# A three-stage network on one core: small tiles widened so that the large buffers begin at multiples of 512 bytes

## The chip, the cores and the metric

The kernel runs on one core of a Trainium2 chip. The metric is the device time in microseconds of one execution; less is better. One execution was also recorded by the profiler, and the lines below come from that record.

## The reference

The reference computes one network of two blocks on 256 tokens of 1024 channels, all in f32. Cut to what matters:

```python
# first block
h = rmsnorm(x, g_mix); proj = h @ w_in                     # 1024 -> 7168 columns
y_a = (rg_lru(xa, forward) + rg_lru(xa, reverse)) * gelu(a_gate) @ w_a_out
z = gate * fftconv(z, k, filt_bias)                        # twice, then @ w_b_out
x = x + (g_a * y_a + g_b * y_b) @ w_o
vals, idx = lax.top_k(softmax(rmsnorm(x) @ w_router).T, 32)
ye = (silu(xe @ w_gate) * (xe @ w_up)) @ w_down            # 16 experts, 1024 -> 2048 -> 1024
x = rmsnorm(x + scatter_add(ye * vals), g_final)
# second block, two layers, each:
x = x + 0.5 * swiglu(x)                                    # 1024 -> 2816 -> 1024
x = x + mixer(x)                                           # recurrent heads, attention heads, pooling
x = x + cross_attention(x, mem)
x = x + 0.5 * swiglu(x)
```

## The kernel before, in words

**Layout of the work.** Tokens or channels lie on the 128 partitions. A weight matrix is read from memory in chunks of 128 rows by 2048 f32 numbers, 8,192 bytes for each partition, in the order in which the products use them. Each chunk is one transfer, issued from SyncE, and it arrives in a buffer named `wc`. Outside the experts, ScalarE rounds the chunk to a high part `wh` (line 303), VectorE subtracts to get the low part `wl` (line 304), and TensorE makes three products of the parts (line 457 with the weights as the moving operand, line 422 with them as the stationary one).

**Stages.** The first block's mixer runs to about 400 us. The experts follow: 16 experts read 24 chunks each, without the split, into 18 buffers in turn (`RING2`): eleven slots of the mixer's pool that are free by then, four `ring` buffers, and three pairs of `wh` and `wl` taken as halves (a row is 4,096 bytes there). Line 1006 makes the gate and up products, line 1030 the down product, lines 1039 to 1043 add the result to `x`. The second block runs from about 1320 us to the end: gated networks with line 457, then mixer, cross attention and a second gated network, for two layers.

**Where tiles lie.** Every tile has one byte address, the same in all partitions. Pools lie one behind the other in the order in which they are made: `const`, `ring`, `spl`, `sm`, `t2`, and then the pool of the present phase (`phmix` for the first block; `late` and the pools on it for the second). A tile is rounded up to 32 bytes and to nothing larger. So the small tiles in `const` and `sm` and the vector tables decide where the large tiles behind them begin. As built, the kernel before has these addresses; the last column is what is left after division by 512:

| tile | pool | begins at byte | past a multiple of 512 |
|---|---|---|---|
| `ident`, 512 bytes | `const` | 16,512 | 128 |
| `neghalf`, 64 bytes | `const` | 17,024 | 128 |
| `x`, 8,192 bytes | `const` | 17,088 | 192 |
| `vec2_0`, `vec2_1` (82 numbers), `gfg`, `rm` | `const` | 25,280 and on | |
| the four `ring` buffers (`wc`), 8,192 bytes each | `ring` | 30,144 and on | 448 |
| three `wh` and three `wl`, 4,096 bytes each | `spl` | 62,912 and on | 448 |
| 48 small tiles, 2,112 bytes together | `sm` | 87,488 and on | |
| five `tmp`, 2,048 bytes each | `t2` | 89,600 and on | 0 |
| `vec1` (229 numbers) or `const2` (1,602 numbers) | `phmix` or `late` | 99,840 | 0 |
| the mixer's slots, among them the eleven that the experts' chunks use | `phmix` | 100,768 and on | 416 |
| `hTh`, `hTl`, `hidh`, `hidl`, `oTh` and the rest of the second block | `late` and on it | 106,272 and on | 288 |

**Order of the work.** Every engine runs its own list, written out by the program, and waits on semaphores; tiles wait for the tiles that had their bytes before. Three places are touched: the constructor of `Net`, `load_vec` (which brings a vector table in by a transfer issued from ScalarE), and `second_setup`, where `gfg` is made.

Of the kernel before, what the change touches and what calls it, by code (L numbers as in the profile page):

```python
# [11 lines left out]
F32 = mybir.dt.float32  # L12
# [7 lines left out]
P = 128  # L20
T = 256
D = 1024
KT = 8
# [3 lines left out]
# ---------------------------------------------------------------- host layout  # L27

def lay_T(w):
    """[K, N] weights for products that give [cols, tokens]: chunks [N/256, 128, 2, K/128, 128]."""  # L30
    K, N = w.shape
    return np.ascontiguousarray(
        w.reshape(K // 128, 128, N // 256, 2, 128).transpose(2, 1, 3, 0, 4)).reshape(N // 256, 128, K * 2)


def lay_A(w):
    """[K, N] weights for products that give [tokens, cols]: chunks [N/512, K/512, 128, 4, 512]."""
    K, N = w.shape
    return np.ascontiguousarray(
        w.reshape(K // 512, 4, 128, N // 512, 512).transpose(3, 0, 2, 1, 4)).reshape(-1, 128, CW)  # L40


def col(v):
    """Channel vectors [..., n*128] -> [128, ... * n]."""
    v = np.asarray(v)
    n = v.shape[-1] // 128
    return np.moveaxis(v.reshape(v.shape[:-1] + (n, 128)), -1, 0).reshape(128, -1)
# [74 lines left out]
def block_diag(w):  # L122
    """[..., 16, 64, 64] -> [128, ..., 8, 128] with pairs of heads on the diagonal."""
# [100 lines left out]
# ---------------------------------------------------------------- the program  # L224
# [6 lines left out]
AHEAD = 2  # L231
# [9 lines left out]
class Net:  # L241
    def __init__(s, ctx, tc, A):
# [6 lines left out]
        s.sm = pool("sm", 2)  # L249
        s.t2 = pool("t2", 5)  # L250
# [4 lines left out]
        s.neghalf = s.const.tile([P, 16], F32, name="neghalf")  # L255
# [3 lines left out]
    # -- helpers  # L259
    @contextmanager  # L260
    def after(s, insts):
        """What is emitted inside issues after these instructions."""
# [17 lines left out]
    def load_vec(s, key, spec, pool=None):  # L280
        off, n = offsets(spec)
        t = (pool or s.const).tile([P, n], F32, name=key)
        s.nc.scalar.dma_start(t, s.A[key])
# [14 lines left out]
    def wsplit(s, w, eng=None):  # L298
        """The two float32r parts of a piece of weights of up to 1024 columns."""
# [13 lines left out]
    def split2(s, src, h, l):  # L313
        """f32 tile -> its two float32r parts, which add up to it exactly."""
# [3 lines left out]
    def rstd(s, src, eps, n=2):  # L318
        """[128, n, 1024] -> 1/sqrt(mean of squares + eps), [128, n]."""
# [11 lines left out]
    def rstd_halves(s, src, eps=1e-6):  # L331
        """As rstd, with the sums taken per half of the columns, as the halves come."""
# [25 lines left out]
    def to_T(s, src, g, h, l, kps=range(4)):  # L358
        """[128 tok, 2, 1024] -> [128 d, 8, 256 tok] in two float32r parts, times g per channel."""
# [14 lines left out]
    def turn(s, g):  # L374
        """The next phase's operand from x, half of the channels at a time."""
# [5 lines left out]
    # a phase's chunks of weights in their order, split AHEAD pieces before their products  # L381
# [24 lines left out]
    def pieces(s, ap):  # L406
        """The halves of a chunk in two parts, from memory or, for None, from the feed."""
# [4 lines left out]
    def lin_T_steps(s, ap, xT, evac, early=False):  # L412
        """One chunk of 256 columns, in two steps: evac(psum [128, 2, 256 tok]). When early, what needs only the
        first half of the channels comes first."""
# [16 lines left out]
    def braid(s, *gens):  # L431
        """Emits several chains' steps, (chain, number of steps), in turn at even paces."""
# [7 lines left out]
    def lin_A_steps(s, aps, xT, kts, evac, cols=512):  # L440
        """Chunks of k-tiles of one block of columns, a step for every half: evac(tok tile, psum [128, cols])."""
# [26 lines left out]
    # -- first block, mixer  # L468
# [6 lines left out]
    def mixer(s):  # L475
# [11 lines left out]
        # filter network; the second layer's output twice, on both halves of the partitions  # L487
# [43 lines left out]
        with after(first):  # L531
            run(sir1)
            run(sir2)
            # [hf + hb | hf - hb] as products with stacked weights, tokens split in even and odd; the sum
            # leaves out the backward filter's first tap
# [11 lines left out]
        def halves(q, xh, xl, out):  # L547
            """Cosine (q=0) or sine transform of one block of columns at the frequencies k and 255-k."""
# [10 lines left out]
        def spectrum(n, K, *sds):  # L559
            """Filter n's kernel in the frequency domain."""  # L560
# [26 lines left out]
        def conv(dst, taps, wname, ch0, b):  # L587
            """Depthwise convolution of a pair of channel tiles: taps are (shift, weight row)."""
# [30 lines left out]
        def lru(d, xa, hA, slots, th=None):  # L619
            """Gates and scan of one direction."""  # L620
# [17 lines left out]
            # one function table after the other  # L638
# [30 lines left out]
        def forward(z, K, us, sds):  # L669
            """Spectrum of z times the filter's, as even and odd combinations, left in K's place."""  # L670
# [39 lines left out]
        def backward(n, j, z, K, xg):  # L710
            """A pair of channel tiles back in time, with the bias and the gate."""
# [13 lines left out]
        def proj(aps, xT, evac):  # L725
            """Chunks of columns, a step for every half."""
# [6 lines left out]
        with after(first):  # L733
            # softplus(-lambda) per channel, times 4
# [53 lines left out]
        # the scan backward in time, with the second gate's and the first branch gate's products  # L788
# [33 lines left out]
        # branch outputs, gated and merged  # L822
# [41 lines left out]
    # -- first block, experts  # L864
# [12 lines left out]
    def router_half(s, b):  # L877
        """The router's products of half of the channels, [experts, tokens], without the norm's factors per token."""
# [12 lines left out]
    def moe(s):  # L891
# [5 lines left out]
        def wload(ap):  # L897
            """A chunk into one of 18 buffers in turn, two into those of the tokens to come; its columns by blocks
            of 512."""
# [17 lines left out]
        # router: softmax over the experts  # L917
# [15 lines left out]
        # the 32 tokens of each expert: those above its 32nd affinity, ties by lowest index  # L933
# [18 lines left out]
        # their slots from 1 on, those above first; the ties that find no room lie past the last slot  # L952
# [9 lines left out]
        # per expert, one token in each slot's column: by the norm's factor, and by the affinity  # L962
# [7 lines left out]
        # gathered tokens, [d, slots], of four experts at a time and halves of the channels  # L970
        xe = {}

        def gather(g, ks, lo, hi):
            """The tokens of the experts lo to hi of a group, for channel tiles of one half."""
# [70 lines left out]
    # -- second block  # L1045
    def ffn(s, l, which, then, first=False):
        nc, A = s.nc, s.A
        with s.tc.tile_pool(name=f"ph{which}{l}", bufs=1) as ph:
# [4 lines left out]
            def finish(f0, n, hs):  # L1053
                """hidden blocks [128 tok, n*128] of both token tiles -> transposed parts."""
# [10 lines left out]
            for i in range(5):  # L1065
# [11 lines left out]
                if i == 0:  # L1077
# [3 lines left out]
                    if first:  # L1081
                        # the first block's last norm, of which the products have only the gain so far
# [31 lines left out]
    def lead(s, steps, n, then):  # L1114
        """The last steps that x takes in a phase; the next phase's operand after n of them and after the last."""
# [14 lines left out]
    def weave(s, lead, fill, n, *gens):  # L1130
        """Emits the steps of several chains in turn, the first with a lead, and n of fill after each round."""
# [9 lines left out]
    def mix_(s, l):  # L1141
# [9 lines left out]
        # time-mix features, [channels, tokens], with the token shift: x9, k, v, r  # L1151
# [38 lines left out]
        # attention features  # L1190
# [39 lines left out]
        # norm of the removal key per head  # L1230
# [10 lines left out]
        # k (1 + (a - 1) k_a); running log decay within chunks  # L1241
# [47 lines left out]
        # AR: per pair of heads and chunk, [scaled key | scaled r] of each head, zeros in the other head's rows  # L1289
# [8 lines left out]
        # pooling features  # L1298
# [34 lines left out]
        # products of the scaled operands, masked: [ab | rb] and [ak | rk], transposed  # L1333
# [12 lines left out]
        # y = [pooling 2, attention 3, time mix 3] tiles  # L1346
# [53 lines left out]
    def inverse(s, ph, O, UV, W64, akv):  # L1400
        """W = (I - ab^T)^-1: 32-blocks by doubling, then the pairs of them. Partitions 0..63 hold the odd
        chunks, 64..127 the even ones."""
# [77 lines left out]
    def chunks(s, ph, V, O, UV, W64, akv, AR, BKt, eC, bn, g, yh, yl):  # L1480
        """The state through the chunks in order, then group norm per head, gain, bonus, gate."""
# [369 lines left out]
```

## Time and profile before

| what | value |
|---|---|
| device time, three executions | 2651.6, 2653.09 and 2656.48 us, median 2653.09 us |
| profiled execution, span from first to last instruction | 2651.9 us |
| instructions | 33,832 |
| TensorE busy | 2276.4 us, 86% |
| VectorE busy | 1187.1 us, 45% |
| ScalarE busy | 863.6 us, 33% |
| GpSimd busy | 250.0 us, 9% |
| moved by DMA | 665.18 MB, 251 GB/s over the span |

For the profiled execution the span is the time that is listed; the median of the three executions is 1.2 us above it. Busy time is an average over stages with different limits, so a change is judged in the stage where it acts: by the chain of waits that ended last there, and by what a single instruction or a single DMA packet takes.

### The profile page before, as it was taken

The numbers are of one execution on the slowest core, as the hardware profiler recorded it, in microseconds if no ns is written. First come the engines' busy times: TensorE is split into PE (matmuls) and PEld (weight loads), VectorE is DVE, ScalarE is ACT, GpSimd is POOL, SyncE is SP. The second block draws the span as 40 slices with busy tenths as digits, with TensorE's granted clock in tenths as the row PEclk, the third lists the DMA queues.
The fourth block names the chain that finished last, engine by engine and source line by source line (L and its number), as shares of the span: only waits on it lengthen the run. The fifth ranks groups of instructions, "written<-read, shape, count | busy, mean of one in ns | idle before, by whom it ended". The sixth has DMA issues, their size and how long they took to land.

```text
span 2651.9 us, 33832 instructions
## 1 busy us (share of the span) xinstructions
PE 2276.4 (86%) x13846; PEld 1503.4 (57%) x13846; DVE 1187.1 (45%) x1714; ACT 863.6 (33%) x1323; POOL 250.0 (9%) x256
## 2 busy tenths in 40 slices
PE   6988889667666667676799999999999999999999
PEld 6987864111111111111178887788888888778887
DVE  6988962000000000000165577655555558765554
ACT  4655420000000000000144455454444445545443
POOL 2333300000000000000000041100000005110000
PEclk9999989877878887778799999999999999999999
DMA  5333579999999999999954434245545443424453
GB/s 212 128 143 120 190 274 416 418 420 418 420 419 420 419 419 420 419 420 419 410 188 176 178 108 147 91 160 183 181 176 189 167 168 125 146 86 164 175 180 122
DMA packets 104636, 665.18 MB, mean 251 GB/s; under 512 B 11808, under 2 KB 12192, under 8 KB 34848
## 3 DMA queue, kind: packets, MB, share of 16 engines
q1 hardware_dynamic: 103328, 660.12, 64.1%
q8 instruction: 109, 1.79, 0.3%
q10 hardware_dynamic: 1008, 1.84, 0.2%
q0 software_dynamic: 144, 1.05, 0.1%
q14 instruction: 47, 0.39, 0.0%
HBM read 661.92 MB, written 1.05 MB: 250 GB/s over the span
## 4 chain that ended last, share of the span: by engine, by line
PE 52%; DMA 33%; DVE 10%; ACT 2%; issue 2%; POOL 1%; SPq 0%; DVEq 0%; ACTq 0%; POOLq 0%
PE lA L457 33%; DMA wc<-in_w_down_dram 13%; DMA wc<-in_w_gate_dram 10%; DMA wc<-in_w_up_dram 9%; PE acc L422 6%; DVE wl L304 2%; PE lA L1659 2%; PE acc L1006 1%; DMA wc<-in_x_wkv_dram 1%; PE trb L1059 1%; PE acc L986 1%; PE acc L309 1%; ACT wh L303 1%; PE acc L552 1%; PE acc L311 1%
## 5 line engine op out<-in xcount | busy, mean ns | idle before, releaser
L304 DVE TENSOR_TENSOR wl<-wc,wh 128x1024 fp32r<-128x1024 f32 (+1 forms) x457 | 566.4, 1243 | 396.6 <-ACT wh L303 382.1
L303 ACT CAST wh<-wc 128x1024 fp32r<-128x1024 f32 (+1 forms) x474 | 492.7, 1041 | 580.0 <-PE lA L457 423.3
L1006 PE MATMUL acc<-wc,xe 128*32 128x512 f32 x2048 | 372.4, 776 | 183.6 <-DMA wc<-in_w_up_dram 95.6
L1006 PEld LDWEIGHTS acc<-wc,xe 128*32 128x32 f32 x2048 | 53.4, 121 | 491.1 <-DMA wc<-in_w_up_dram 225.0
L1019 DVE TENSOR_TENSOR tmp<-tmp,acc 128x512 f32<-128x512 f32 x16 | 11.0, 688 | 537.5 <-PE acc L1006 529.3
L457 PE MATMUL lA<-wh,hTl 128*128 128x512 f32 (+1 forms) x864 | 241.5, 396 | 0.0
L457 PE MATMUL lA<-wh,hTh 128*128 128x512 f32 (+1 forms) x864 | 236.8, 395 | 3.2 <-ACT hTh L369 3.2
L457 PE MATMUL lA<-wl,hTh 128*128 128x512 f32 (+1 forms) x864 | 232.9, 391 | 2.3 <-DVE wl L304 2.3
L1030 PE MATMUL acc<-wc,tmp 128*32 128x512 f32 x1024 | 169.8, 723 | 70.2 <-DMA wc<-in_w_down_dram 56.3
L457 PEld LDWEIGHTS lA<-wh,hTh 128*128 128x128 f32 x864 | 162.3, 190 | 40.7 <-ACT hTh L369 5.2
L457 PEld LDWEIGHTS lA<-wl,hTh 128*128 128x128 f32 x864 | 162.2, 189 | 38.0 <-DVE wl L304 3.0
L1018 ACT ACTIVATE tmp<-acc 128x512 f32<-128x512 f32 x16 | 9.6, 597 | 519.7 <-PE acc L1006 519.7
L457 PEld LDWEIGHTS lA<-wh,hTl 128*128 128x128 f32 x864 | 159.5, 190 | 31.0
L1043 DVE TENSOR_TENSOR x<-x,acc 128x512 f32<-128x512 f32 x64 | 44.0, 688 | 270.6 <-PE acc L1042 270.6
L1030 PEld LDWEIGHTS acc<-wc,tmp 128*32 128x32 f32 x1024 | 30.0, 121 | 193.7 <-DMA wc<-in_w_down_dram 115.9
L1039 ACT COPY tmp<-acc 128x512 f32<-128x512 f32 x32 | 18.7, 585 | 320.3 <-PE acc L1030 320.3
L422 PE MATMUL acc<-hTh,wl 128*128 128x256 f32 x640 | 95.9, 291 | 24.3 <-DVE wl L304 20.7
L422 PE MATMUL acc<-hTh,wh 128*128 128x256 f32 x640 | 100.2, 297 | 3.3 <-ACT tmp L555 1.4
L422 PEld LDWEIGHTS acc<-hTh,wl 128*128 128x128 f32 x640 | 85.5, 195 | 26.6 <-DVE wl L304 22.2
L457 PE MATMUL lA<-wl,hidh 128*128 128x512 f32 x352 | 98.3, 398 | 0.0
L457 PE MATMUL lA<-wh,hidh 128*128 128x512 f32 x352 | 96.9, 397 | 0.0
L457 PE MATMUL lA<-wh,hidl 128*128 128x512 f32 x352 | 96.7, 396 | 0.0
(451 smaller groups left out, 3002.0 us busy)
## 6 DMA issues: line engine op xcount, KB each, us to landing
wc<-in_w_up_dram SPq DMA_DIRECT2D x117, 1024.0 KB, 18.6
wc<-in_w_gate_dram SPq DMA_DIRECT2D x102, 1024.0 KB, 19.8
wc<-in_w_down_dram SPq DMA_DIRECT2D x102, 1024.0 KB, 18.6
wc<-in_ffn_wi_dram SPq DMA_DIRECT2D x88, 1024.0 KB, 4.8
wc<-in_ffn_wo_dram SPq DMA_DIRECT2D x40, 1024.0 KB, 4.7
wc<-in_w_in_dram SPq DMA_DIRECT2D x39, 1024.0 KB, 4.8
wc<-in_w_gate_dram SPq DMA_DIRECT2D x52, 512.0 KB, 13.8
wc<-in_w_down_dram SPq DMA_DIRECT2D x52, 512.0 KB, 16.2
```

The costliest lines, as they stand in the source:

```text
L303: s.nc.scalar.copy(h[:, :n], w)
L304: (eng or s.nc.vector).tensor_tensor(l[:, :n], w, h[:, :n].bitcast(F32), op=OP.subtract)
L309: mm(out, a[0], b[0], start=start, stop=False)
L311: mm(out, a[1], b[0], start=False, stop=stop)
L422: s.nc.tensor.matmul(ps[:, c, :], w[:, k, :], x[:, k, :], start=i + k == 0, stop=i == 2 and k == KT - 1)
L457: s.nc.tensor.matmul(pss[t], x[:, n + kk, t * P:t * P + P], w[:, kk, :], start=n + kk + i == 0, stop=i == 2 and n + kk == kts - 1)
L552: nc.tensor.matmul(ps, part[:, 2 * q + rr, :], x[:, rr, :], start=i == 0, stop=i == 2)
L986: nc.tensor.matmul(ps[:, i, :], s.x[:, t, k * P:(k + 1) * P], oh[:, t, 4 * g + lo:4 * g + hi].rearrange("p e c -> p (e c)"), start=t == 0, ...
L1006: nc.tensor.matmul(ps[32 * j:32 * j + 32, :], xe[e // 4, k // 4][:, k % 4, es], c(j), start=k == 0, stop=k == KT - 1)
L1030: nc.tensor.matmul(py[b][32 * j:32 * j + 32, :], ht[:, t, 32 * j:32 * j + 32], c(j), start=t == 0, stop=t == 3)
L1043: nc.vector.tensor_tensor(s.x[:, t, cs], s.x[:, t, cs], ps, op=OP.add)
L1659: s.nc.tensor.matmul(pss[t], x[:, n + kk, t * P:t * P + P], w_[:, kk, :], start=n + kk + i == 0, stop=i == 2 and n + kk == KT - 1)
```

## The change

`neghalf` grows from 16 to 96 numbers, of which the first 16 are used as before. `gfg` grows from 8 to 120, of which 8 are used. A vector table is rounded up to a multiple of 128 numbers (82 to 128, 229 to 256, 1,602 to 1,664); its transfer still writes the `n` numbers of the table. A tile `even` of 112 numbers, which nothing writes or reads, is taken from `sm`. No instruction is added, removed or moved in the source. Comments and docstrings are dropped too, and code after the constructor's start stands two lines further down than before.

```diff
         s.sm = pool("sm", 2)
+        s.sm.tile([P, 112], F32, name="even", bufs=1)
         s.t2 = pool("t2", 5)
...
-        s.neghalf = s.const.tile([P, 16], F32, name="neghalf")
+
+        s.neghalf = s.const.tile([P, 96], F32, name="neghalf")[:, :16]
         nc.gpsimd.memset(s.neghalf, -0.5)
         s.x = s.const.tile([P, 2, D], F32, name="x")
...
         off, n = offsets(spec)
-        t = (pool or s.const).tile([P, n], F32, name=key)
-        s.nc.scalar.dma_start(t, s.A[key])
+        t = (pool or s.const).tile([P, -(-n // P) * P], F32, name=key)
+        s.nc.scalar.dma_start(t[:, :n], s.A[key])
...
-        s.gfg = s.const.tile([P, KT], F32, name="gfg")
+        s.gfg = s.const.tile([P, P - KT], F32, name="gfg")[:, :KT]
```

## Rows read from the trace of the kernel before

**Rows 1.** The page: span, busy time, the chain that ended last by engine and line.
```profile
span 2651.9 us, 33832 instructions
...
PE 2276.4 (86%) x13846; PEld 1503.4 (57%) x13846; DVE 1187.1 (45%) x1714; ACT 863.6 (33%) x1323; POOL 250.0 (9%) x256
...
PE 52%; DMA 33%; DVE 10%; ACT 2%; issue 2%; POOL 1%; SPq 0%; DVEq 0%; ACTq 0%; POOLq 0%
PE lA L457 33%; DMA wc<-in_w_down_dram 13%; DMA wc<-in_w_gate_dram 10%; DMA wc<-in_w_up_dram 9%; PE acc L422 6%; DVE wl L304 2%; PE lA L1659 2%; PE acc L1006 1%; DMA wc<-in_x_wkv_dram 1%; PE trb L1059 1%; PE acc L986 1%; PE acc L309 1%; ACT wh L303 1%; PE acc L552 1%; PE acc L311 1%
```

**Rows 2.** Stages by windows: width, busy us (instructions) by engine, PEclk, DMA share, GB/s.
```profile
core 0: us, PE busy (x) PEld busy (x) DVE busy (x) ACT busy (x) POOL busy (x), PEclk, DMA share, GB/s
...
530.00:1260.00 730.00, 501.67 (x2502) 91.97 (x2502) 50.94 (x74) 25.66 (x50) 7.04 (x24) 0.80 1.02 419
...
1327.00:1790.00 463.00, 445.85 (x3177) 368.21 (x3176) 290.48 (x443) 226.43 (x372) 58.20 (x61) 0.99 0.42 149
1790.00:2115.00 325.00, 325.00 (x1448) 261.76 (x1447) 175.32 (x185) 149.42 (x177) 1.39 (x2) 1.00 0.51 181
```

**Rows 3.** The chain that ended last, from 480 to 1290 us, by line.
```profile
by line: DMA wc<-in_w_down_dram 39.0%; DMA wc<-in_w_gate_dram 32.1%; DMA wc<-in_w_up_dram 28.3%; PE acc L1030 0.6%; issue 0.3%; PE trb L1014 0.2%; PE acc L1006 0.1%; DVE tmp L1019 0.1%; PE trb L1022 0.1%; SPq L904 0.1%; SPq L908 0.0%; DVEq 
```

**Rows 4.** DMA from 398 to 1293 us: packets by size; queue: packets, MB, share.
```profile
DMA packets 59920, 374.93 MB, mean 419 GB/s; under 512 B 6659, under 2 KB 6659, under 8 KB 21704
...
q1 hardware_dynamic: 59884, 374.42, 101.4%
```

**Rows 5.** DMA from 2243.3 to 2243.5 us, `memT` into `tmp`, same columns.
```profile
DMA packets 38, 0.08 MB, mean 389 GB/s; under 512 B 0, under 2 KB 0, under 8 KB 38
...
q1 hardware_dynamic: 38, 0.08, 99.8%
```

**Rows 6.** DMA from 5.6 to 6.0 us, the second half of `x`.
```profile
DMA packets 73, 0.15 MB, mean 374 GB/s; under 512 B 0, under 2 KB 0, under 8 KB 73
...
q1 hardware_dynamic: 73, 0.15, 97.4%
```

**Rows 7.** DMA from 2243.6 to 2243.8 us, `memT` again, with semaphore packets.
```profile
DMA packets 44, 0.08 MB, mean 379 GB/s; under 512 B 7, under 2 KB 7, under 8 KB 44
...
q1 hardware_dynamic: 44, 0.08, 99.1%
```

**Rows 8.** Lines 1059 and 366, transposes of `tmp` and of `x`: min/median/max ns.
```profile
L1059 PEld LDWEIGHTS trb<-ident,tmp x176: 137/140/144, 1344.9 to 2587.3; 128*128 128x128 f32 x176
L1059 PE MATMUL trb<-ident,tmp x176: 270/272/301, 1345.1 to 2587.4; 128*128 128x128 f32 x176
...
L366 PEld LDWEIGHTS trb<-ident,x x128: 137/140/143, 1308.0 to 2457.4; 128*128 128x128 f32 x128
L366 PE MATMUL trb<-ident,x x128: 270/272/329, 1308.0 to 2457.5; 128*128 128x128 f32 x128
```

**Rows 9.** Lines 1019 and 1043, VectorE on `tmp` and on `x`, same columns.
```profile
L1019 DVE TENSOR_TENSOR tmp<-tmp,acc x16: 686/689/689, 413.0 to 1294.4; 128x512 f32<-128x512 f32 x16
...
L1043 DVE TENSOR_TENSOR x<-x,acc x64: 686/688/690, 437.6 to 1317.6; 128x512 f32<-128x512 f32 x64
```

**Rows 10.** Lines 1039 and 1782, ScalarE into `tmp` and into `oTh`, same columns.
```profile
L1039 ACT COPY tmp<-acc x32: 585/585/586, 418.9 to 1313.6; 128x512 f32<-128x512 f32 x32
...
L1782 ACT CAST oTh<-acc x8: 585/585/587, 1762.0 to 2432.4; 128x512 fp32r<-128x512 f32 x8
```

**Rows 11.** Lines 1042, 1006 and 457, matmuls of 512 columns, same columns.
```profile
L1042 PE MATMUL acc<-tmp x128: 592/592/1222, 436.5 to 1316.5; 128*128 128x512 f32 x128
...
L1006 PE MATMUL acc<-wc,xe x2048: 589/617/1063, 392.7 to 1293.3; 128*32 128x512 f32 x187
...
L457 PE MATMUL lA<-wh,hTh x864: 335/397/1415, 1316.6 to 2582.4; 128*128 128x512 f32 x154, 128*128 128x384 f32 x19
```

**Rows 12.** DMA issues of the whole span: count, KB each, median us to landing.
```profile
x<-in_x_dram SPq DMA_DIRECT2D x2, 512.0 KB, 6.5
...
vec<-in_vec_dram ACTq DMA_DIRECT2D x1, 114.5 KB, 2.0
```

## The prediction

> **What bounds the kernel now.** The page comes first: its chain that ended last is TensorE for 52% and DMA for 33%, and of the DMA part 13, 10 and 9% are the experts' three weight matrices; the largest single item is line 457 with 33% [rows 1]. The windows by stage then say where each rules: from 530 to 1260 us the DMA share is 1.02 at 419 GB/s while TensorE is busy for 501.67 of 730 us, and in the second block, from 1790 to 2115 us for instance, TensorE is busy for all 325 us and the DMA share is 0.51 [rows 2]. The chain cut to 480 to 1290 us is DMA for 39.0 + 32.1 + 28.3 = 99.4% [rows 3]. So there are two places in which an address could matter: what one row costs a DMA engine on its way into `wc` (experts), and what one instruction costs TensorE, with ScalarE and VectorE in front of it (second block). The rest of my reading looks for pairs, in the kernel before, of one operation on a tile that already begins at a multiple of 512 bytes (`tmp`) and on one that doesn't (`x` at 192, `oTh` at 288, `wc` at 448 or 416).
>
> **What the change does to the addresses.** `neghalf` takes 384 bytes instead of 64, so `x` goes from 17,088 to 17,408 = 34 x 512. The two `vec2` tables take 512 each instead of 352, `gfg` 480 instead of 32: `ring` goes to 31,232 = 61 x 512, and `spl`, 32,768 further, to a multiple as well. `even` adds 448 to the 2,112 bytes of `sm`: `t2` starts at 91,136 = 178 x 512. `vec1` takes 1,024 instead of 928 and `const2` 6,656 instead of 6,432: the mixer's slots begin at 102,400 and `hTh` at 108,032, both multiples. The mixer's tiles move by 1,632 bytes and the second block's by 1,760, 128 apart. Before, the former lie at 416 and the latter at 288, so their ends never lie closer than 128 bytes, and the shift can make an overlap of 128 bytes vanish but no new one: no wait for an old tile's bytes is added.
>
> **Instructions: nothing.** None is added, removed or moved, on SP's and POOL's queues either. `neghalf` is filled and read in its first 16 numbers as before, `gfg` in its 8, and the tables' transfers move the same bytes; `vec1` lands after 2.0 us, before `x` at 6.5 us, which the first products need anyway [rows 12]. `even` has no instruction. The cost is 0.
>
> **DMA rows.** In a stretch in which every packet is a row of 2,048 bytes (MB divided by packets shows it), the queue's share gives the time of a row. `memT` into `tmp`, offset 0: 99.8% of 16 engines x 0.2 us = 3.194 us for 38 rows, 84.0 ns [rows 5]. `x`, offset 192: 97.4% of 16 x 0.4 us = 6.234 us for 73 rows, 85.4 ns [rows 6]. So an unaligned start costs at most 1.4 ns a row, and the second pair was taken in the busy start of the kernel, which may be all of it. From 398 to 1293 us the queue moved 59,884 packets, 6,659 of them semaphore writes, so 53,225 rows [rows 4], 3,327 for each of 16 engines: at 1.4 ns that is 4.7 us. That is the near bound. The far bound is that everything in a row that does not grow with its bytes goes away. Semaphore packets take 9 ns: 99.1% of 3.2 us is 3.171 us for 37 rows and 7 of them, and (3.171 - 37 x 0.084) / 7 = 0.009 [rows 7]. The expert stretch took 101.4% of 16 x 895 us = 14,520 us, less 60 us for semaphores 14,460 us; if each of its rows had 2,048 bytes at 84.0 ns that would be 4,471 us for 109.0 MB, and the other 265.4 MB took 9,989 us, 37.6 ns per 1,000 bytes. A row of 2,048 bytes then has 77.1 ns of bytes and 6.9 ns of fixed cost, and 3,327 x 6.9 ns = 23 us. I take 0, because 84.0 and 85.4 ns lie at the near end, and keep -4.7 and -23 us for the range.
>
> Here a rule of the Trainium skill would give another result. DMA: Bandwidth & Descriptors, section How a descriptor splits into AXI transactions, says that a descriptor which doesn't start on a 256-byte boundary fetches from the boundary below and pays for the unused bytes; it speaks of reads, and here the unaligned side is written. By the page alone, as an estimate: rows at 448 and 416 past a multiple of 512 would carry 192 and 160 bytes more, 2.3 to 2.7% of the stretch, some 20 to 24 us. The trace disagrees as far as it goes: `x` begins 192 bytes past such a boundary too, which by the rule is 9% of a 2,048-byte row, and its rows took 1.7% more than aligned ones [rows 5, 6].
>
> **TensorE.** The same transpose of 128 columns, from `tmp` (line 1059) and from `x` (line 366), takes 270 and 272 ns at the minimum and the median in both, and the weight load 137 and 140 in both [rows 8]. Difference 0. For 512 columns there is no exact pair: line 1042 with both operands in `tmp` takes 592 ns at the least, line 1006 with `wc` at 448 or 416 takes 589 [rows 11]. The 3 ns may belong to the 128 columns of weights against 32; taken as a price of alignment they bound a loss at 0.5%. A gain is bounded by the transposes: 0 of 272 ns. I take 0, the exact pair.
>
> **VectorE and ScalarE.** The subtraction and the product of 512 columns take 688 to 689 ns at the median on `tmp` and on `x` [rows 9]; ScalarE's copy out of PSUM takes 585 into `tmp` and 585 into `oTh` [rows 10]. TensorE does wait for line 304, which is 2% of the chain [rows 1], 53 us; one nanosecond in 688 there would be 53 / 688 = 0.08 us. I take 0.
>
> **Sum.** 2651.9 us of the profiled execution + 0 (instructions) + 0 (rows) + 0 (engines) = 2651.9 us. The median of the three executions is 1.2 us above this span, so the forecast is 2653.0 us. The three reach from 2651.6 to 2656.5 us, so 0.2%, 5.3 us, is about what can be told from no change.
>
> **The rivals.**
> *Rows get cheaper.* In the expert stretch each row loses its cost of an odd start. The stretch is DMA for 99.4% [rows 3], so all of it reaches the end: 4.7 us by the pair of rows, 23 us if the whole fixed cost was the odd start; 2648 to 2630 us. For it: DMA is the bound there, nothing hides it, and the pair is for 2,048-byte rows, not for a saturated stream of 8,192-byte ones. Against it: 1.4 ns at most, and in a busy stretch. Chance 0.14, two thirds of it below 10 us. That the page's rule holds, which is its far end, I give 0.03 of these.
> *The operands collide.* Slower, by one mechanism: after the change `hTh` and `hidh` begin at the same place modulo 512 as `wh` and `wl`, where before they were at 288 and 448; if TensorE's weight loads and moving reads at equal places disturb each other, line 457 pays. The price is 3 of 592 ns, 0.5% [rows 11], on TensorE's 52% of the chain [rows 1], 1379 us: +7 us, 2660 us. It decides (over 0.2%) once line 457's median goes from 397 to above 398.5 ns [rows 11]. Against it: `wc`, `wh` and `wl` share an offset already, and line 1059 with `tmp` at 0 is not slower than line 366 [rows 8]. Chance 0.08.
> *It doesn't do what it says.* `even` is neither written nor read; if the allocator drops it, `t2` begins at 90,688 and the mixer's and second block's tiles begin 64 past a multiple, while `x`, `ring` and `spl` are aligned. Then `tmp` loses the place that it has now. By the pairs [rows 8 to 10] this costs 0: 2653 us too. Chance 0.08, counted with the forecast.
>
> **How the numbers follow.** Forecast (with the last rival) 0.78, cheaper rows 0.14, collision 0.08. The forecast's own range is what the executions show, 2649.5 to 2657.5 us. Faster by over 0.2%: of the 0.14 some 0.12, as the near end lies at the edge, and 0.02 of the forecast by scatter, 0.14. Slower: 0.08 and 0.02 by scatter, 0.10. Same: 0.76. The range reaches to the near half of both rivals, 2645 to 2660 us, and leaves out 0.07 below and 0.06 above.
>
> **What would show it.** In the profile after: 33,832 instructions but for a few; the expert stretch at 419 GB/s and a DMA share of 1.01 to 1.02; an `x` row at 84 to 86 ns; line 457 at 397, line 1043 at 688, line 1782 at 585 ns at the median. A rate above 421 GB/s from 530 to 1260 us would show cheaper rows; a median of line 457 above 398.5 ns the collision. The prediction is wrong if a saturated stream of long rows feels its start where short rows don't, or if two reads at a time feel what single ones don't.

## The result, and the profile after

The kernel after takes 2612.42 us at the median of four executions (2610.84 to 2613.56), the kernel before, run beside it, 2652.35 us (2649.1 to 2656.48). The ratio is 0.9843, with a 95% interval of 0.9829 to 0.9857. That is faster by 40 us, or 1.6%, where 2653 us with a range of 2645 to 2660 had been forecast: the prediction was wrong. The smaller part of the gain lay among its rivals, with a small chance; the larger part it had taken as 0.

The page after: span, busy time, the chain by engine and by line (the rows before are [rows 1]).

```profile
span 2611.5 us, 33832 instructions
...
PE 2246.7 (86%) x13846; PEld 1502.5 (58%) x13846; DVE 1190.5 (46%) x1714; ACT 864.4 (33%) x1323; POOL 248.6 (10%) x256
...
PE 52%; DMA 32%; DVE 10%; ACT 2%; issue 2%; POOL 1%; SPq 0%; DVEq 0%; ACTq 0%; POOLq 0%
PE lA L459 32%; DMA wc<-in_w_up_dram 11%; DMA wc<-in_w_down_dram 11%; DMA wc<-in_w_gate_dram 8%; PE acc L424 6%; PE lA L1661 3%; DVE wl L306 2%; PE acc L1008 1%; PE acc L1032 1%; PE trb L1061 1%; DMA wc<-in_ffn_wi_dram 1%; PE acc L988 1%; ACT wh L305 1%; PE acc L311 1%; PE acc L554 1%
```

The instructions are the same on every engine, and the shares of the chain hardly move: both of its large parts got shorter. TensorE's busy time falls by 29.7 us with the same number of matmuls, so single ones got cheaper. Windows by stage after (columns as in [rows 2]):

```profile
530.00:1260.00 730.00, 498.57 (x2536) 89.18 (x2528) 50.06 (x73) 24.53 (x48) 7.11 (x24) 0.82 1.01 426
...
1790.00:2115.00 325.00, 325.00 (x1484) 268.36 (x1483) 178.28 (x184) 149.56 (x173) 0.70 (x1) 1.00 0.53 186
```

The experts' stretch now moves 426 GB/s instead of 419. In the second window TensorE is busy all the time at the same granted clock of 1.00, and does 1,484 matmuls where it did 1,448 [rows 2]. Single instructions after (min/median/max ns; every line number is 2 higher than before; before: [rows 8 to 11]):

```profile
L459 PE MATMUL lA<-wh,hTh x864: 331/389/667, 1301.3 to 2543.9; 128*128 128x512 f32 x154, 128*128 128x384 f32 x19
...
L1008 PE MATMUL acc<-wc,xe x2048: 589/617/1062, 391.6 to 1277.9; 128*32 128x512 f32 x187
...
L1044 PE MATMUL acc<-tmp x128: 592/592/1222, 437.1 to 1300.8; 128*128 128x512 f32 x128
...
L368 PE MATMUL trb<-ident,x x128: 270/272/331, 1292.8 to 2422.6; 128*128 128x128 f32 x128
...
L1045 DVE TENSOR_TENSOR x<-x,acc x64: 686/689/690, 438.2 to 1301.4; 128x512 f32<-128x512 f32 x64
...
L1784 ACT CAST oTh<-acc x8: 586/587/587, 1741.1 to 2398.1; 128x512 fp32r<-128x512 f32 x8
```

One line stands out: line 457, now 459, fell from 397 to 389 ns at the median. Transposes, VectorE, ScalarE and the experts' gate and up products (line 1006, now 1008) kept their times within 2 ns. Line 422, now 424, with 256 columns, got slower, from 281 to 283 ns at the median (its rows stand at experiment 12). The first and last starts also cut the span into stages. The first gate or up product came at 392.7 us and comes at 391.6; the last scatter product started at 1316.5 us and starts at 1300.8. So the mixer gave 1.1 us, the experts 14.6 us (923.8 to 909.2) and the second block 24.7 us (1335.4 to 1310.7). The mixer's 1.1 us is no more than it differs by from run to run below (390.0 to 392.4 us).

The second block's pace in the chain of waits of before and of after, from 1790 to 2115 us (start us, us, what):

```profile
1839.16 22.03 PE lA L457 x94
```

```profile
1838.97 21.36 PE lA L459 x94
```

An unbroken run of 94 such matmuls took 22.03 us, 234.4 ns each, and takes 21.36 us, 227.2 ns each. The groups of line 457 on `hTh`, `hTl`, `hidh`, `hidl`, `oTh` and `oTl` have 3 x 864 + 3 x 352 + 3 x 64 = 3,840 matmuls, 288 of them with 384 columns; for the other 3,552, 7.2 ns each are 25.6 us, about the second block's gain of 24.7 us.

### The profile page after: what moved, and what is told of

It is laid out like the page before. It is cut to its first block, busy times and chain, and to the rows that moved or that the text cites. A ratio compares the mean times of both kernels' runs of the same rounds, so it can differ in the third digit from the quotient of the medians.

```text
span 2611.5 us, 33832 instructions
## 1 busy us (share of the span) xinstructions
PE 2246.7 (86%) x13846; PEld 1502.5 (58%) x13846; DVE 1190.5 (46%) x1714; ACT 864.4 (33%) x1323; POOL 248.6 (10%) x256
## 3 DMA queue, kind: packets, MB, share of 16 engines
q10 hardware_dynamic: 1008, 1.84, 0.2%
## 4 chain that ended last, share of the span: by engine, by line
PE 52%; DMA 32%; DVE 10%; ACT 2%; issue 2%; POOL 1%; SPq 0%; DVEq 0%; ACTq 0%; POOLq 0%
PE lA L459 32%; DMA wc<-in_w_up_dram 11%; DMA wc<-in_w_down_dram 11%; DMA wc<-in_w_gate_dram 8%; PE acc L424 6%; PE lA L1661 3%; DVE wl L306 2%; PE acc L1008 1%; PE acc L1032 1%; PE trb L1061 1%; DMA wc<-in_ffn_wi_dram 1%; PE acc L988 1%; ACT wh L305 1%; PE acc L311 1%; PE acc L554 1%
## 5 line engine op out<-in xcount | busy, mean ns | idle before, releaser
L305 ACT CAST wh<-wc 128x1024 fp32r<-128x1024 f32 (+1 forms) x474 | 493.0, 1042 | 560.0 <-PE lA L459 402.0
L459 PE MATMUL lA<-wh,hTh 128*128 128x512 f32 (+1 forms) x864 | 230.6, 387 | 3.3 <-ACT hTh L371 3.3
L1032 PE MATMUL acc<-wc,tmp 128*32 128x512 f32 x1024 | 162.5, 705 | 66.9 <-DMA wc<-in_w_down_dram 53.2
L1041 ACT COPY tmp<-acc 128x512 f32<-128x512 f32 x32 | 18.8, 586 | 312.1 <-PE acc L1032 312.1
```

The source lines that it names most:

```text
L305: s.nc.scalar.copy(h[:, :n], w)
L459: s.nc.tensor.matmul(pss[t], x[:, n + kk, t * P:t * P + P], w[:, kk, :], start=n + kk + i == 0, stop=i == 2 and n + kk == kts - 1)
L1032: nc.tensor.matmul(py[b][32 * j:32 * j + 32, :], ht[:, t, 32 * j:32 * j + 32], c(j), start=t == 0, stop=t == 3)
```

## The experiments

The theory after the result had two parts, given here as they stood at the end (that 256 bytes is the period came with experiments 5 to 7). **TensorE:** a matmul takes two operands, the stationary one, which is loaded first, and the moving one; what counts is where the first begins *relative to* the second, modulo 256 bytes. **DMA:** in a saturated stream a row costs more when its place in the on-chip buffer is no multiple of 256 (called odd below; even is a multiple). The rivals were that each tile's own place counts (a multiple of 512), that other engines' reads and writes cause it, and that the place of `x` has a part in it.

Experiments 1 to 8 are the kernel after with further padding in front of one group of tiles. Unwritten pools `pr` before `ring` and `ps` before `spl`, a wider `even`, and `more` numbers behind a vector table do it. The places are bytes past a multiple of 512; "late" stands for `hTh`, `hidh` and `oTh` of the second block, "slots" for the mixer's tiles that the experts' chunks use. Each time is the median of four executions, and each ratio is to runs of before on the same chip beside them; stages, rates and single instructions are those of one profiled execution. "Line 457" in the table is that line under the number that it has in each kernel, 457 to 461.

| kernel | late / wh, wl / ring / slots | line 457 median ns | experts, second block us | GB/s, 530 to 1230 us | time us | ratio, 95% |
|---|---|---|---|---|---|---|
| before | 288 / 448 / 448 / 416 | 397 | 923.8, 1335.4 | 419 | 2652.35 | |
| after | 0 / 0 / 0 / 0 | 389 | 909.2, 1310.7 | 426 | 2612.42 | 0.9843 [0.9829, 0.9857] |
| 1 | 288 / 0 / 0 / 0 | 395 | 909.0, 1330.5 | 426 | 2634.29 | 0.9929 [0.9914, 0.9943] |
| 2 | 32 / 32 / 0 / 0 | 389 | 911.2, 1311.9 | 425 | 2616.20 | 0.9858 [0.9843, 0.9872] |
| 3 | 0 / 448 / 0 / 0 | 394 | 909.7, 1332.3 | 425 | 2635.43 | 0.9935 [0.992, 0.995] |
| 4 | 0 / 0 / 448 / 416 | 389 | 916.1, 1312.7 | 422 | 2624.19 | 0.9889 [0.9873, 0.9906] |
| 5 | 256 / 0 / 128 / 64 | 389 | 916.8, 1310.7 | 422 | 2618.29 | 0.987 [0.9855, 0.9884] |
| 6 | 64 / 0 / 256 / 128 | 394 | 912.7, 1329.8 | 424 | 2638.96 | 0.9949 [0.9931, 0.9968] |
| 7 | 128 / 0 / 64 / 256 | 392 | 910.5, 1330.5 | 426 | 2634.41 | 0.9927 [0.9912, 0.9942] |
| 8 | as after, `x` at 192 | 389 | 909.1, 1314.2 | 426 | 2616.91 | 0.9861 [0.9844, 0.9878] |
| 9 | 448 / 448 / 448 / 416 | 389 | 923.0, 1314.5 | 419 | 2628.95 | 0.9906 [0.989, 0.9923] |
| 12 | as after, `wh`, `wl` shifted by use | 389 | 909.6, 1310.9 | 426 | 2612.69 | 0.9855 [0.9837, 0.9872] |

**1. Only the late tiles back to 288.**

```diff
-    def load_vec(s, key, spec, pool=None):
+    def load_vec(s, key, spec, pool=None, more=0):
...
-        t = (pool or s.const).tile([P, -(-n // P) * P], F32, name=key)
+        t = (pool or s.const).tile([P, -(-n // P) * P + more], F32, name=key)
...
-        s.C2 = s.load_vec("const2", CONST2, s.late)[1]
+        s.C2 = s.load_vec("const2", CONST2, s.late, 72)[1]
```

> The changed kernel with the second block's tiles alone put back to 288 bytes past a multiple of 512 (hTh, hidh, oTh; everything else stays at 0). Between the two profiles the mixer of the first block took 1 us of the gain of 40.4, the experts 14.7, the second block 24.7, and line 457's median fell from 397 to 389 ns. Theory A (the place of the stationary operand counts, or its place against the moving one): line 457's median back at 397 ns, expert stretch still at 426 GB/s, time 2612 + 25 = 2637 us. Theory B (only the moving operand wh, wl counts): 389 ns and 2612 us. Rival C (the whole gain hangs on the DMA rows, TensorE only follows): 389 ns and 2612 us.

Line 459 of this kernel, min/median/max ns:

```profile
L459 PE MATMUL lA<-wh,hTh x864: 333/395/668, 1301.7 to 2562.4; 128*128 128x512 f32 x154, 128*128 128x384 f32 x19
```

The second block's gain is gone but for 4.9 us, and the experts' gain stays whole: two separate effects.

**2. Late tiles and `wh`, `wl` all at 32.** `more` of `const2` is 8; besides

```diff
+        pool("ps", 1).tile([P, 8], F32, name="ps")
         s.spl = pool("spl", 3)
...
-        s.sm.tile([P, 112], F32, name="even", bufs=1)
+        s.sm.tile([P, 232], F32, name="even", bufs=1)
```

> The changed kernel with wh, wl and the second block's tiles all 32 bytes past a multiple of 512, so that both operands of line 457 begin at the same odd place; ring (and mT in it), the mixer's slots and x stay at 0. Theory A1 (the two operands' places against each other count): line 457 at 389 ns, 2612 us plus about 3 us for line 1659, whose mT is at 0 while wh is at 32 (its 389 to 393 ns would rise by 8 on 384 matmuls). Theory A2 (the stationary operand off a multiple of 64 costs): line 457 at 397 ns, line 1659 unchanged, 2637 us. Theory B (moving operand off its place costs): 397 ns, line 1659 slower too, 2640 us. In the expert stretch 3 of 18 buffers are off by 32: 426 GB/s if only odd rows pay their own share less 0.2%, about 425.

```profile
L460 PE MATMUL lA<-wh,hTh x864: 333/389/668, 1302.4 to 2546.2; 128*128 128x512 f32 x154, 128*128 128x384 f32 x19
...
L1662 PE MATMUL lA<-wh,mT x256: 388/396/582, 1583.1 to 2390.0; 128*128 128x512 f32 x128
```

In the second block no operand of line 460 begins at a multiple of 64, and it takes 389 ns all the same, because both are at 32. `mT`, which stayed at 0, now lies 32 off, and line 1662 went from 393 to 396. Equal places are what counts, not even ones.

**3. Only `wh`, `wl` back to 448.** `ps` of 112 numbers, `even` of 128.

> The changed kernel with wh and wl alone put back to 448 bytes past a multiple of 512 (7 x 64), all else at 0. Theory B (the moving operand must begin at a multiple of 512): line 457 at 397 ns, 2637 us. Theory A1 with places counted modulo 512: 397 ns too. Theory A1 with places counted modulo 64, and A2: 389 ns, 2612 us. The experts' half-chunks go into these buffers: if rows pay each for itself, the expert stretch loses a sixth of its gain, 2.4 us; if one odd row in a stream slows all, up to 14.7 us.

```profile
L460 PE MATMUL lA<-wh,hTh x864: 333/394/667, 1301.0 to 2563.6; 128*128 128x512 f32 x154, 128*128 128x384 f32 x19
```

The median of line 457, here 460, is 394 ns, and 396 to 398 with `oTh` and `oTl`: a shift of the moving operand costs about what one of the stationary operand costs. The second block is back at 1332.3 us.

**4. Only the rows' places back to those of before.** `pr` of 112 numbers, `ps` of 16, `more` of `vec1` 104.

> The changed kernel with ring back at 448 and the mixer's slots back at 416, the two places where 15 of the experts' 18 buffers lie; wh, wl, x, tmp and the second block stay at 0. Theory D (rows that begin at an odd place take longer in a saturated stream): the expert stretch back at 419 to 420 GB/s, time 2612 + 12 to 15 = 2624 to 2627 us, line 457 at 389 ns. Rival E (the experts' gain came from TensorE or from tmp and x, the DMA rate followed): 426 GB/s and 2612 us.

```profile
530.00:1260.00 730.00, 505.98 (x2520) 90.51 (x2512) 50.11 (x73) 24.81 (x48) 7.11 (x24) 0.78 1.02 422
```

The matmuls stay at 389 ns. The experts lose 6.9 of their 14.6 us and the rate falls to 422 GB/s, where 419 to 420 had been expected: 15 of the 18 buffers are odd, and `spl` is still even. In the packet records 64% of the rows of 8,192 bytes take over 309 ns, against 92% in before, so the even buffers in between spare some of the odd rows their cost. The four executions' median lost 12 us, the profiled one 8.

**5, 6 and 7. The three groups at 64, 128 and 256, in turn.** `pr`, `ps`, `more` of `vec1` and of `const2` are 32, 96, 16, 64 (5), 64, 64, 32, 16 (6) and 16, 112, 64, 32 (7).

> The changed kernel with the second block's tiles at 256, ring (mT too) at 128 and the mixer's slots at 64 past a multiple of 512; wh, wl, x and tmp stay at 0. So the stationary operand stands 256 from the moving one in line 457's second block and 128 from it in line 1659. If the two places must agree modulo 512: line 457 at 394 to 397 ns and line 1659 at 394, the second block 22 us longer. If modulo 256: line 457 at 389 and line 1659 at 394. If modulo 128: both at 389. Rows into ring (128) and slots (64): if a row must start at a multiple of 512 or 256, the stretch from 530 to 1230 us runs at 422 GB/s as in the run with 448 and 416, 10 to 12 us lost; if a multiple of 64 is enough, 426. Times: 2612 + 22 + 11 = 2645 us (512 for both), 2623 us (256 for both), 2612 us (64 or 128).

> As the run before with the places turned: second block at 64, ring at 256, mixer's slots at 128. Modulo 512: line 457 at 394 to 397 ns, line 1659 at 394; modulo 256: line 457 at 394 to 397, line 1659 at 389 to 393; modulo 64: both fast. Rows: at 256 in ring fast and at 128 in the slots slow if a row wants a multiple of 256, both slow if 512, both fast if 128 or 64. Times: 2645 us (512 for both), 2641 us (256 for both), 2612 us (64).

> The third turn: second block at 128, ring at 64, mixer's slots at 256. Modulo 512 or 256: line 457 at 394 to 397 ns; modulo 128: 389 there and 394 in line 1659 (64). Rows: with 11 of 18 buffers at 256 the expert stretch runs at 425 to 426 GB/s if a multiple of 256 is enough, at 422 if not. Times: 2645 us (512 for both), 2637 us (256 for both).

For TensorE 256 apart is as good as equal (389 ns), 128 and 64 apart are not (392 and 394). For DMA 256 is as good as 0: slots at 256 took 309.0 ns a row in the packet records (7), ring at 256 309.2 (6). Slots at 64 and 128 took 312.1 and 311.2, ring at 128 313.4. But in 7 the ring's four buffers at 64 took 309.1, as if even: a few odd buffers among even ones cost nearly nothing.

**8. Only `x` back to 192.** `neghalf` of 144 numbers, `pr` of 80.

> The changed kernel with x alone put back to 192 past a multiple of 512; all else at 0. x is read by transposes and by VectorE and is never paired with wh or wl in one matmul, and its two rows of 2,048 bytes arrive before the first product. Theories A1 and D: nothing, 2612 us, line 457 at 389 ns, 426 GB/s. Rival (every large tile's place counts by itself): 2 to 5 us slower.

The rate and line 459 stay as after, the lines on `x` within 2 ns. The profiled execution lost 3.5 us in the second block, and the ratio's interval overlaps that of after, so no effect of `x` is shown, and one of up to 0.4% isn't excluded: the rival's 2 to 5 us stay open.

**9. One part alone, on the kernel before.** Its `const2` tile grows by 40 numbers (`more` as in 1, the table's transfer into `t[:, :n]`), and nothing else.

> The kernel before with one thing changed: the tile of const2 is 160 bytes wider, so hTh, hidh and oTh go from 288 to 448 past a multiple of 512, which is the place of wh and wl. Every large tile stays off the multiples. Theory (only the place of the stationary operand relative to the moving one counts for TensorE, only the places of the rows for DMA): line 457's median goes from 397 to 389 ns, the second block loses about 25 us (1335 to 1311), the experts stay at 419 GB/s and 924 us; in all about 2627 us, ratio 0.990 to 0.991. Rival (what counts is that each tile begins at a multiple of 512 or 256): nothing is a multiple here, so 397 ns and 2652 us, ratio 1.000.

Windows, then line 457, then the pace in the chain:

```profile
530.00:1260.00 730.00, 498.33 (x2500) 89.99 (x2500) 50.95 (x74) 24.88 (x50) 7.04 (x24) 0.81 1.02 419
```

```profile
L457 PE MATMUL lA<-wh,hTh x864: 331/389/669, 1315.5 to 2561.9; 128*128 128x512 f32 x154, 128*128 128x384 f32 x19
```

```profile
1831.77 21.33 PE lA L457 x94
```

No large tile is at a multiple of 512 or 256 except `tmp` and the vector tables, the rate is before's 419 GB/s, and the matmuls are as fast as in the kernel after. 160 bytes of padding give 23.4 of the 40 us, which is the theory's number (2627 expected, 2628.95 measured). That each tile's own place is what counts for line 457 is refuted.

**10. The matmuls alone.** The network is left out, and there is one execution; a group is 64 matmuls, `a` and `b` the starts of its operands, and each group runs twice.

```python
for i in range(n):
    for t in range(2):
        w = a + 128 * ((2 * i + t) % 16)
        m = b + cols * (i % (2048 // cols))
        nc.tensor.matmul(ps[t], st[:, w:w + 128], mv[:, m:m + cols], start=i == 0, stop=i == n - 1)
```

> The network is left out: only groups of 64 matmuls of one stationary tile and one moving tile, with both starts set by the group, all other engines idle, 512 columns first and then 256, each group twice. Theory (TensorE's two reads by themselves, relative place modulo 256): 389 ns at 512 columns where the starts are equal or 256 apart, whether at 0, 64 or 128; 394 to 398 at 32, 64, 96, 160, 192, 224 and 320 apart, 392 to 395 at 128, the same when the moving tile is shifted instead. At 256 columns the equal starts are not the best: 283 against 279 to 282. Rival (what costs the time is the other engines' reads and writes in the same memory meanwhile): alone, all groups take the same, within 1 ns.

Rows by tile, 512 columns. The starts (stationary, moving) are aa 0, 0; ab 32, 0; ac 64, 0; ad 96, 0; ae 128, 0; af 160, 0; ag 192, 0; ah 224, 0; ai 256, 0; aj 64, 64; ak 0, 64; then three with 256 columns, aa 0, 0, ao 0, 192 and ac 64, 0.

```profile
L40 PE MATMUL aaw<-mv,st x256: 387/389/796, 9.5 to 512.2; 128*128 128x512 f32 x128
L40 PE MATMUL abw<-mv,st x128: 392/395/397, 54.5 to 497.6; 128*128 128x512 f32 x128
L40 PE MATMUL acw<-mv,st x128: 393/394/398, 69.4 to 482.7; 128*128 128x512 f32 x128
L40 PE MATMUL adw<-mv,st x128: 391/397/400, 84.3 to 467.8; 128*128 128x512 f32 x128
L40 PE MATMUL aew<-mv,st x128: 390/393/404, 99.3 to 452.8; 128*128 128x512 f32 x128
...
L40 PE MATMUL afw<-mv,st x128: 388/394/399, 114.2 to 437.9; 128*128 128x512 f32 x128
...
L40 PE MATMUL agw<-mv,st x128: 388/392/398, 129.1 to 423.0; 128*128 128x512 f32 x128
...
L40 PE MATMUL ahw<-mv,st x128: 388/394/397, 143.8 to 408.3; 128*128 128x512 f32 x128
...
L40 PE MATMUL aiw<-mv,st x128: 388/389/396, 158.7 to 393.4; 128*128 128x512 f32 x128
L40 PE MATMUL ajw<-mv,st x128: 387/389/398, 173.2 to 378.9; 128*128 128x512 f32 x128
L40 PE MATMUL akw<-mv,st x128: 388/392/394, 187.8 to 364.4; 128*128 128x512 f32 x128
...
L40 PE MATMUL aan<-mv,st x128: 277/283/283, 512.4 to 754.1; 128*128 128x256 f32 x128
...
L40 PE MATMUL aon<-mv,st x128: 276/276/286, 618.5 to 648.0; 128*128 128x256 f32 x128
...
L40 PE MATMUL acn<-mv,st x128: 276/280/282, 527.6 to 738.8; 128*128 128x256 f32 x128
```

With all other engines nearly idle the pattern of the kernel is there: 389 ns at equal starts (0, 64; 128, 128 gave 389 too) and at 256 apart, 392 to 397 elsewhere. The kernel before had 288 - 448, which is 96 modulo 256: group ad has its 397 ns. The first starts give the pace as well: the 64 matmuls of ad took 99.3 - 84.3 = 15.0 us, 234 ns each, and those of ai 173.2 - 158.7 = 14.5 us, 227 ns each, as in the kernels before and after. So no other engine is needed for it. That TensorE's two reads of the memory get in each other's way is the likely reason, but not shown. At 192 apart (ag and ak) it was 392 instead of the 394 to 398 expected. With 256 columns equal starts are the *slow* case, 283 ns against 276 to 281 elsewhere; there the starts aren't the whole of it, since group ac has a median of 281 ns the first time (527.6 to 535.0 us) and of 276 the second (731.7 to 738.8 us).

**11. The rows alone.** The network is left out, and there is one execution; chunks of 1 MB go into 16 buffers in turn, and no engine reads them.

```python
a = starts[i % len(starts)] // 4
t = ring.tile([P, 2176], F32, name=name, tag="ring")
for c in range(0, 2048, cols):
    nc.sync.dma_start(t[:, a + c:a + c + cols], w[n // 8 % 16, n % 8][:, c:c + cols])
```

> The network is left out: only transfers of 1 MB of the gate matrix into 16 buffers in turn, 32 of them for each start (0, 448, 256, 128, 64, 32, 192, every other one at 448, every fourth at 448), the round twice, with no engine reading the buffers. Theory (the write of a row by DMA itself costs more from a start that is no multiple of 256): 426 GB/s at 0 and 256, about 419 at the others, between the two for every other one, near 426 for every fourth. Rival (what costs the time is that TensorE reads the same buffers meanwhile, from odd places): all groups move the same, within 1 GB/s.

Windows, one for each start of the first round: 0, 448, 256, 128, 64, 32, 192, every other chunk at 448, every fourth (width, POOL, PEclk, DMA share, GB/s):

```profile
10.00:78.00 68.00, 0.00 (x0) 1.00 1.01 427
89.00:157.00 68.00, 0.00 (x0) 1.00 1.01 422
168.00:236.00 68.00, 0.00 (x0) 1.00 1.01 427
247.00:315.00 68.00, 0.00 (x0) 1.00 1.01 423
326.00:395.00 69.00, 0.00 (x0) 1.00 1.01 422
406.00:475.00 69.00, 0.00 (x0) 1.00 1.01 420
486.00:554.00 68.00, 0.00 (x0) 1.00 1.01 422
565.00:633.00 68.00, 0.00 (x0) 1.00 1.01 426
644.00:711.00 67.00, 0.00 (x0) 1.00 1.01 427
```

0 and 256 move 427 GB/s, the other starts 420 to 423, and the second round gave the same within 1. A row took 309.0 ns at 0 and 256 and 313.1 to 314.5 elsewhere. With nothing reading the buffers, it is the write of the row itself and not an engine's reads. Alternating starts cost 0.9 ns a row at most, and in their packet records 8 to 20% of all rows take over 309 ns, where half of the rows are odd. A chunk is 128 rows on 16 DMA engines, eight rows on each (one semaphore packet comes for every eight rows in [rows 4]), so eight odd rows follow one another there as well: the loss shows in full only where chunk after chunk is odd.

**12. The places turned for line 424.** Line 422, now 424, has 256 columns, and the change brought its operands to equal places, the slow case of experiment 10; before and after:

```profile
L422 PE MATMUL acc<-hTh,wh x640: 274/281/583, 14.3 to 2220.9; 128*128 128x256 f32 x160
```

```profile
L424 PE MATMUL acc<-hTh,wh x640: 274/283/582, 12.7 to 2188.5; 128*128 128x256 f32 x160
```

In the kernel after, the split halves now go 64 bytes into wider tiles where line 424 reads them.

```diff
-        h = s.spl.tile([P, 1024], F32R, name="wh")
-        l = s.spl.tile([P, 1024], F32R, name="wl")
+        h = s.spl.tile([P, 1088], F32R, name="wh")[:, sh:sh + 1024]
+        l = s.spl.tile([P, 1088], F32R, name="wl")[:, sh:sh + 1024]
...
-            yield s.piece() if ap is None else s.wsplit(w[:, 1024 * c:1024 * c + 1024])
+            yield s.piece() if ap is None else s.wsplit(w[:, 1024 * c:1024 * c + 1024], sh=16)
```

> The kernel after, with wh and wl read and written 64 bytes into their tiles (which are 256 bytes wider) where the weights are the stationary operand (line 424), and at the start of their tiles as before where they are the moving one. Theory: what the matmuls alone showed for 256 columns holds in the kernel: line 424's median goes from 283 to 279 ns, a group of 64 takes 15.1 us for every 128 instead of 15.7, 4% less. Line 424 is 28.6% of the chain up to 392 us and 2.8% of it from 1300 us on, 149 us together; 4% of that is 6 us, so about 2606 us against 2612, and lines 459 at 389 ns, the experts at 909 us as after. Rival: in the mixers other engines set the pace and the shorter matmuls only wait longer: 279 ns too, but 2611 to 2613 us. Third: the odd starts slow ScalarE's or VectorE's writes of wh and wl (lines 305 and 306), then it is slower than 2613.

```profile
L424 PE MATMUL acc<-hTh,wh x640: 276/281/583, 13.0 to 2187.7; 128*128 128x256 f32 x160
...
L424 PE MATMUL acc<-zh,wh x64: 276/276/384, 321.6 to 343.5; 128*128 128x256 f32 x64
```

The medians fell from 283 to 281 ns (with `zh`, to 276), where 279 had been expected, and the 6 us of the theory didn't come: the time is that of after, 2612.69 us. The mixer was 1.6 us shorter in the profiled execution, which is hardly more than it differs by among the other runs (390.7 to 392.7 us).

## Why the prediction was wrong, by its own steps

**Instructions and addresses: right.** 33,832 instructions, and the tiles lie where the prediction put them.

**DMA rows: wrong, and this is the first failed step.** It took 0 because rows of 2,048 bytes took nearly the same at 192 and at 0 [rows 5, 6], and carried that over to a saturated stream. The measured price there is 4.8 ns for a row of 8,192 bytes (313.8 to 309.0 ns) and 3.8 for 4,096 (162.9 to 159.1). With 38,216 long and 15,045 short rows [rows 4] on 16 engines that is 11.5 + 3.6 = 15 us; the experts gave 14.6. This is the rival of cheaper rows, between its bounds of 4.7 and 23 us, and its sign came: 426 GB/s, above 421. The value chosen, 0, was not it. The pair's 1.4 ns was no price of the start: of the 73 rows that begin in the stretch of [rows 6] one took 180 ns, and the median is 84. The same stretch has 78 rows of 84 ns each in after, with `x` at 0, and 77 rows of 84 ns each in experiment 9, with `x` at 192. So an odd row costs nothing more there; the price appears only in the saturated stream, which the pair couldn't show. A better pair stood in the trace of before. Packet records of rows of 8,192 bytes (ns; share of them at exactly 309):

```
before, 1330 to 2640 us (second block, ring at 448)   84% at 309
before,  530 to 1230 us (experts, ring 448, slots 416)  8% at 309, median 313
after,   530 to 1230 us (experts, all aligned)        100% at 309, median 309
after,  1330 to 2640 us (second block, ring at 0)     84% at 309
```

At half the load (a DMA share of 0.42 to 0.53 in the windows) the share at 309 is 84% whether the ring is odd or even. The condition that the prediction named itself ("if a saturated stream of long rows feels its start where short rows don't") is what happened, but by the load and not by the length: the saturated rows of 4,096 bytes pay too.

**The rule of the Trainium skill: the period is right, the size is not.** Experiments 7 and 11 agree with the Trainium skill (DMA: Bandwidth & Descriptors, How a descriptor splits into AXI transactions) that 256 bytes is the boundary, and show it for the written side, where the section speaks of reads. Its size, as the prediction worked it out from the unused bytes, disagrees: by that a start at 32 wastes least and one at 192 or 448 six times as much, and measured were 420 GB/s at 32 and 422 at 192 and 448; the experts gave 14.6 us where that estimate was 20 to 24. The 0.03 that it was given was too little for the period, and fair for the amount.

**TensorE: wrong, the second failed step, and the larger one.** "I take 0, the exact pair": the pair was two transposes of 128 columns, whose operands `ident` (at 128), `tmp` (at 0) and `x` (at 192) have unequal places in both cases (128 and 64 apart), so the pair couldn't set equal places against unequal ones. So the price of 0 for TensorE's instructions was the wrong term: with 512 columns it is 8 of 397 ns in a single record and 7.2 ns in the pace, 24.7 us in the second block. "For 512 columns there is no exact pair" was wrong as well. The trace of before held one for the places, line 1659, where `mT` and `wl` are both at 448:

```profile
L1659 PE MATMUL lA<-wl,mT x128: 387/389/504, 1605.6 to 2422.8; 128*128 128x512 f32 x128
```

389 ns there against line 457's 397 [rows 11], in one kernel, of one shape. It is a hint and not more, for the same line's 256 products with `wh`, at 448 too, have 393 at the median, before and after.

**The rival "operands collide" had the place and the cause, and the sign reversed.** It said that line 457 depends on `hTh` and `wh` being at the same place. They do matter to each other, but equal places are the fast case. The Trainium skill (TensorE: Matmul & The Clock Gate, Step-by-step: what each phase is for) says that the weights and the moving operand come by two independent read ports. As far as time goes they aren't independent in experiments 9 and 10: the place of one against the other is worth 3 to 8 ns on 389.

**VectorE and ScalarE: right.** 689 and 587 ns against 688 and 585 [rows 9, 10]; nothing there.

**What stays open.** Why equal places modulo 256 help with 512 columns and hurt with 256, and how even rows in between take away the cost of odd ones. No run here looks inside either. Experiment 4's 12 us for 15 odd buffers and experiment 5's 6 us differ by more than their rows explain (916.1 and 916.8 us in the experts).

## What to carry to other kernels

Where TensorE is the bound with 512 moving columns in float32r and 128 columns of weights, the form measured here, put the stationary and the moving tiles at the same place modulo 256 bytes; where a DMA stream is saturated, put its buffers at multiples of 256. Look for the price in the same kind of stretch as the one in question: the same shape, length of row and load, since a cost that is absent in sparse work was 1.6% of a row in a saturated stream here, and one that the transposes of 128 columns didn't show was 3% of a matmul's pace. Pad one group alone on the old kernel: 160 bytes of it told two effects apart here.

## What the runs showed of the hardware

- At a granted clock of 1.00 a matmul of 128 x 512 float32r takes 389 ns when stationary and moving operands begin 0 or 256 bytes apart modulo 512, and 392 to 397 ns at 32, 64, 96, 128, 160, 192 and 224 apart (experiment 10); in an unbroken run that was 227 ns each at 256 and 234 ns at 96 apart. With 256 columns it is 283 ns when equal and 276 to 281 otherwise.
- A saturated stream of 8,192-byte rows moved 427 GB/s into starts at multiples of 256 and 420 to 423 GB/s into others. With every other buffer odd it moved 426 GB/s (experiment 11). At half the load the same rows took 309 ns in 84% of the cases, with an odd ring as with an even one.
